# Other PSUM banks for the attention behind the decode's small products, and later squares of the first half's attention result

## The chip, the core and the metric

The kernel runs on one core of one Trainium2 chip. Five engines work side by side, each through its own instructions in order: TensorE (PE, with its weight loads shown apart as PEld), VectorE (DVE), ScalarE (ACT), GpSimd (POOL) and SyncE (SP), which here only issues transfers. Matrix products are written to PSUM, eight banks of 128 x 512 words of 32 bits; the other engines read them from there. The metric is the device time of one execution in microseconds. The program has been measured in several runs, and one more execution was recorded by the profiler.

## The reference

One layer of a decoder that mixes two kinds of heads. It serves a prompt of 1024 tokens and, with the same weights, 8 samples of one token each, whose past of 8192 tokens lies in paged caches. All is in 32-bit floats, D is 1024, there are 8 attention heads of 64.

```python
def fox_attend(q, k, v, cq, ck, qpos, kpos):
    s = jnp.einsum('bqhd,bkhd->bhqk', q, k).astype(jnp.float32) * (ATT_HEAD_DIM ** -0.5)
    s = s + (cq.astype(jnp.float32).transpose(0, 2, 1)[:, :, :, None]
             - ck.astype(jnp.float32).transpose(0, 2, 1)[:, :, None, :])
    s = jnp.where(kpos[None, :] <= qpos[:, None], s, -jnp.inf)
    p = jax.nn.softmax(s, axis=-1).astype(v.dtype)
    return jnp.einsum('bhqk,bkhd->bqhd', p, v)
...
def merge_heads(att, sgu, g_att_out, g_sgu_out, w_o):
    return jnp.concatenate([rmsnorm(att, g_att_out), rmsnorm(sgu, g_sgu_out)], axis=-1) @ w_o
```

Ahead of this stand the projections to q, k, v, a forget logit (its running sum is cq and ck) and the gating heads; behind it stand the cross-attention to 256 memory tokens and a gated MLP with a short convolution. The samples do the same with `fox_attend` over their cached keys and values. The change touches the attention of the prompt, the first norm in `merge_heads`, and the places in PSUM of three small products of the samples' attention.

## The kernel before

**Two streams.** The prompt's work is written as generators that yield a cost; after each yield the main loop deals out pieces of the samples' work (`decode`, then `sample_rest`) at a pace set for each phase. So the samples' instructions lie between the prompt's. A scheduler of the language then places the instructions on the engines; `tc.issue_after(x)` and the helper `behind(engine)` say behind which instruction something has to stand. `lastexp[0]` is the newest exponential of the attention.

**Phases.** First the projections (to about 260 us); then the attention of the first 512 rows (`att0`, to about 372 us), dealt together with the memory's keys and values and the gating of the first half; then the attention of the second 512 rows (`att1`, to about 505 us); then, for each half, the output projection, the cross-attention and the MLP, with the rest of the decode beside them; at the end the rest of the samples' layer.

**One attention.** `attention(hf)` runs over four pairs of heads, two blocks of 256 rows each. `setup` brings q and k of a pair into the form that the products need: it loads qn (L733), k and v (L739, L740) and, in the second half, the keys of the first half from `ks_d` (L769, L770); transposes (L750, L779), copies on ScalarE (L757, L784) and differences on VectorE (L774, L788) follow. `setup` of a pair runs during the pair before; the first pair of the second half is set up within the first attention. `scores` makes the score rows of 128 queries (L807, L809, L811) in a ba bank, their maximum on VectorE (L816; L813 in the first half) and the exponential on ScalarE (L817; L814). `turn` transposes the probabilities (L836) and copies them back (L843, or L841 on VectorE). `values` multiplies by v (L852) and copies the result (L861); `back` transposes that (L872), and VectorE divides it by the sum of the exponentials (L863, L874) into the tile `att`.

**PSUM.** Of the eight banks four are `ba` (in the second attention two tiles of two banks), two `bb`, one `ms` and one `dv`. A tile of a tag waits until the last reader of the tile that had its bank is done. `B3` gives the tiles of `turn`, `values` and `back`: each third goes to `ms`, the others to `bb`. The matrix products of the memory use `ba` and, for each third tile, `bb`. The decode's small products all go to `ms`: the gates' cumulative sum (`gates`, L1409, read by VectorE in L1411), the transpose of the maxima (`soft_all`, L1459, read in L1462) and the spread of the maximum (`soft_exp`, L1472, read in L1474 before the exponential L1475).

**The end of an attention.** `close` is a generator in three steps: the squares of the four 128 x 512 tiles of `att`, summed by ScalarE (`ssq_into`, L230); the reciprocal root (`rstd_of`, VectorE L222, GpSimd L223); and the multiplication of the four tiles by it (VectorE, L958) with two stores to `an_d` on SP's queue (L960). `beside` runs a generator and takes one step of another behind its yields of given numbers. The first half's `close` is begun directly behind the first attention, and its two other steps stand behind the yields 0 and 2 of the second attention. The output projection of the first half reads `an_d` (`merge_in`), which the second attention calls at its fourth pair of heads.

Of the kernel before, what the change touches and what calls it, by code (L numbers as in the profile page):

```python
# [63 lines left out]
M3 = 3  # L64
# [14 lines left out]
def build(nc, tc, ctx, a, phases=None):  # L79
# [27 lines left out]
    def nm(s):  # L107
        cnt[0] += 1
        return f"{s}_{cnt[0]}"
# [16 lines left out]
    def sm(shape, tag, bufs=2, dt=F32):  # L126
        return small.tile(shape, dt, tag=tag, bufs=bufs, name=nm(tag))
# [13 lines left out]
    def BB():  # L141
        return psum.tile([P, 512], F32, tag="bb", bufs=2 + MB, name=nm("bb"))
# [8 lines left out]

    def MS():
        return BB() if MB else psum.tile([P, 512], F32, tag="ms", bufs=1, name=nm("ms"))

    def DV():
        return psum.tile([P, 512], F32, tag="dv", bufs=1, name=nm("dv"))
# [69 lines left out]
    def ssq_into(dst, src):  # L226
        n = src.shape[-1]

        j = src if n > 512 else tpool.tile([P, 512], BF16, tag="junk", bufs=1, name=nm("junk"))[: src.shape[0], :n]
        nc.scalar.activation(j, src, AF.Square, accum_out=dst)  # L230
# [495 lines left out]
    def attention(hf, late=None, at=3):  # L726
        nk = 4 * (hf + 1)
        att = []
# [94 lines left out]
        turns = [0.0, 0]  # L823

        def B3():
            turns[1] += 1
            return MS() if turns[1] % M3 == M3 - 1 else BB()

        def turn(p_, pts, n, ii):

# [116 lines left out]
    def close(hf, att):  # L947

        ssa = sm([P, 4], "ssa", 1)
        for i in range(4):  # L950
            ssq_into(ssa[:, i : i + 1], att[i // 2][:, i % 2, :])
        yield
        r = rstd_of(ssa, AW, 4, "ra")
        yield
        for b2 in range(2):
            for i in range(2):
                t = att[b2][:, i, :]
                nc.vector.tensor_scalar(t, t, r[:, b2 * 2 + i : b2 * 2 + i + 1], None, op0=ALU.mult)  # L958
            t0 = hf * 4 + b2 * 2
            nc.sync.dma_start(an_d[t0 * P : (t0 + 2) * P, :].rearrange("(c p) d -> p c d", p=P), att[b2])  # L960
        yield

    def beside(main, steps, at):

        n = 0
        while True:
            try:
                t = next(main)
            except StopIteration as e:
                return e.value  # L970
            yield t
            if n in at:
                next(steps)
            n += 1
# [381 lines left out]
    lastexp = []  # L1356
# [3 lines left out]
    def behind(e):  # L1360

        return tc.issue_after(last[e]) if e in last else nullcontext()


    def decode():
# [36 lines left out]
        def gates(b, A):  # L1402
            tot = sm([P, 8], "tot", 2)
            nc.vector.tensor_tensor(
                tot, A.rearrange("p (h k) -> p h k", k=64)[:, :, 63], lfz[:, b * 8 : b * 8 + 8], op=ALU.add
            )
            ps = MS()
            with behind(ENG.PE):
                mmul(ps[:, :8], suf, tot, start=True, stop=True)  # L1409
            dt_ = dec("dec").rearrange("p (k h) -> p k h", h=8)  # L1410
            nc.vector.tensor_tensor(  # L1411
                dt_, ps[:, :8].unsqueeze(1).broadcast_to((P, 64, 8)), A.rearrange("p (h k) -> p k h", k=64), op=ALU.subtract
            )
            return dt_
# [39 lines left out]
            return pm  # L1454

        def soft_all(b, pm):
            ps = MS()
            with behind(ENG.PE):
                nc.tensor.transpose(ps[:8, :P], pm, ident)  # L1459
            with tc.high_priority():  # L1460
                m1 = sm([8, 1], "m1", 2)
                nc.vector.tensor_reduce(m1, ps[:8, :P], axis=AX.X, op=ALU.max)  # L1462
                nc.vector.tensor_tensor(mT[:, b : b + 1], m1, snT[:, b : b + 1], op=ALU.max)
                dg = dgs[b % 2]
                nc.vector.tensor_scalar(dg[:8, :], ident[:8, :8], mT[:, b : b + 1], None, op0=ALU.mult)
            return dg

        def soft_exp(b, st, dg):
            s = st[1]
            ps = MS()  # L1470
            with behind(ENG.PE):
                mmul(ps[:, :8], ones, dg, start=True, stop=True)  # L1472
            with tc.high_priority():
                nc.vector.tensor_tensor(s, s, ps[:, :8].unsqueeze(1).broadcast_to((P, 64, 8)), op=ALU.subtract)  # L1474
                nc.scalar.activation(s, s, AF.Exp)  # L1475
                nc.vector.tensor_reduce(lps[:, b, :], s.rearrange("p k h -> p h k"), axis=AX.X, op=ALU.add)
# [366 lines left out]
    def prompt():  # L1843
        def fill():
            yield from pmem()
            if not G0R:
                yield from gating(0)

        got, ahead = [], []
        att1 = attention(1, lambda: got.append(merge_in(0)))  # L1850
        att0, fill0 = attention(0, (lambda: next(att1)) if LT < 4 else None, LT), fill()

        def early():
            next(att0)
            next(fill0)

        yield from p1(early)
        phase[0] = "att0"
        att = yield from mix(att0, fill0, MIXR)
        def load_x(hf):  # L1860
            xt = []
            for i in range(4):
                t = U([P, D])
                nc.sync.dma_start(t, a["x"][(hf * 4 + i) * P : (hf * 4 + i + 1) * P, :])
                xt.append(t)
            return xt

        if LT > 3:
            yield next(att1)
        ending = close(0, att)  # L1870
        next(ending)
        phase[0] = "att1"
        ba_pool(True)
        if G0R:
            att = yield from mix(gating(0), att1, 1 / G0R)
        else:
            att = yield from beside(att1, ending, (0, 2))
        ba_pool(False)
        ending = close(1, att)
        next(ending)  # L1880
        ends = []
        for hf in range(2):
            if not got and hf == 0:
                got.append(merge_in(hf))
            xt = []
            phase[0] = f"mid{hf}"
            if hf == 0:
                mh, ml = yield from beside(merge(*got.pop()), ending, (3, 7))
            else:
                mh, ml = yield from ahead[0]  # L1890
            if ends:
                yield from ends.pop()
            sq = yield from out_proj(a["w_o"], mh, ml, xt, partial(load_x, hf))
            if hf == 0:
                ys = yield from mix(cross(xt, sq), gating(1), 0.05)
            else:
                ys = yield from cross(xt, sq)
            phase[0] = f"ffn{hf}"
            sq = yield from ffn(hf, xt, ys, (lambda: ahead.append(merge(*merge_in(1))) or ahead[0]) if hf == 0 else None)
            held[0] = False  # L1900
            ends.append(final(hf, xt, sq))
        yield from ends.pop()
# [121 lines left out]
```

## Time and profile before

| | |
|---|---|
| Runs, device time | 1807.55, 1807.73, 1808.47 us; median 1807.73 us |
| The profiled execution | 1812.65 us, of which its span is 1810.9 us |
| Granted clock of TensorE, mean of the span | 0.987 |
| Moved | 521.06 MB, mean 288 GB/s |

The profile is of one execution, whose time stands beside its span above: what lies around the span is 1.75 us. The median of the runs is 4.92 us below that execution's time. All times of instructions below are microseconds from the start of the span. In the rows of a timeline the columns are the start, the duration, the engine, the line, the operation and its tiles (result <- operands, buffer numbers left out); a bracket gives how long the engine was idle before and what released it. Rows with x2 or more are neighbouring instructions taken together.

### The profile page before, as it was taken

Reading aid. Unit: us, or ns where it says so; the run is one execution under the profiler, and the core shown is the slowest. Engines: PE = TensorE matmul, PEld = TensorE weight load, DVE = VectorE, ACT = ScalarE, POOL = GpSimd, SP = SyncE. Lnnn points to the kernel's source line nnn. Section 1 sums busy time; section 2 is a strip of 40 time slices with the busy share of each in tenths; the row PEclk is TensorE's granted clock in tenths of the full one; section 3 lists DMA queues with packets and bytes.
Section 4 is the critical chain, followed back from the end, with each engine's and each line's share of the span. In section 5 each row is a group of like instructions: output and inputs, shape, how many; then the busy total and the mean of one; then the engine's idle time right before and its main releaser. Section 6 shows DMA issues by size and latency. Waiting matters only on the chain.

```text
span 1810.9 us, 25097 instructions
## 1 busy us (share of the span) xinstructions
PE 1741.1 (96%) x9637; PEld 1295.4 (72%) x9637; DVE 1398.3 (77%) x1729; ACT 735.3 (41%) x1378; POOL 503.7 (28%) x461
## 2 busy tenths in 40 slices
PE   8999999878999899999999999999989999999997
PEld 5887776656677667777777777766676678767775
DVE  4689668987788887999999899888875549855344
ACT  6332265465633544433323244235353323232332
POOL 1252333522133323233232132433322111001110
PEclk9999999988999999999999999999999999999999
DMA  8886889786596876689788788979878677568982
GB/s 300 305 296 228 303 303 341 251 276 195 214 403 259 344 306 269 261 285 342 298 293 320 291 310 309 382 286 361 315 273 318 241 278 263 182 262 292 360 313 82
DMA packets 157074, 521.06 MB, mean 288 GB/s; under 512 B 20874, under 2 KB 40842, under 8 KB 124186
## 3 DMA queue, kind: packets, MB, share of 16 engines
q0 software_dynamic: 57168, 341.14, 49.7%
q1 hardware_dynamic: 92874, 165.73, 26.5%
q10 hardware_dynamic: 6912, 12.59, 1.8%
q8 instruction: 76, 1.25, 0.3%
q14 instruction: 44, 0.36, 0.1%
HBM read 495.47 MB, written 23.93 MB: 287 GB/s over the span
## 4 chain that ended last, share of the span: by engine, by line
PE 50%; issue 8%; DMA 8%; DVE 7%; POOL 2%; ACT 1%; POOLq 0%; DVEq 0%; ACTq 0%
PE ba L272 6%; PE ba L274 6%; PE ba L273 6%; DMA kv<-cache_v,io 6%; PE dv L1487 3%; PE bb L272 3%; PE bb L273 3%; PE bb L274 3%; DVE s L1439 1%; DVE kv L1435 1%; DVE wl L236 1%; PE dv L331 1%; DMA kv<-cache_k,io 1%; PE dv L1763 1%; POOL kv L1419 1%
## 5 line engine op out<-in xcount | busy, mean ns | idle before, releaser
L235 ACT ACTIVATE wh<-wr 128x1024 fp32r<-128x1024 f32 (+2 forms) x220 | 228.2, 1043 | 451.2 <-PE ba L273 143.2
L236 DVE TENSOR_TENSOR wl<-wr,wh 128x1024 fp32r<-128x1024 f32 (+2 forms) x220 | 263.1, 1202 | 173.8 <-PE ba L274 57.1
L1419 POOL DMA_INDIRECT kv<-cache_k,io x128 | 196.7, 1537 | 578.5 <-DVE s L1439 323.1
L1435 DVE TENSOR_TENSOR kv<-kv,d 128x1024 f32<-128x1024 f32 (+1 forms) x156 | 258.1, 1682 | 32.6 <-DMA kv<-cache_k,io 27.3
L1439 DVE TENSOR_REDUCE s<-kv 128x16 f32<-128x1024 f32 (+1 forms) x156 | 258.6, 1676 | 0.0
L1481 POOL DMA_INDIRECT kv<-cache_v,io x128 | 167.6, 1310 | 258.7 <-PE dv L1487 179.9
L273 PE MATMUL ba<-u,wh 128*128 128x512 f32 x528 | 208.5, 395 | 2.4 <-DVE u L239 2.4
L272 PE MATMUL ba<-u,wh 128*128 128x512 f32 x528 | 209.5, 397 | 0.0
L274 PE MATMUL ba<-u,wl 128*128 128x512 f32 x528 | 209.1, 396 | 0.0
L272 PE MATMUL ba<-wh,u 128*128 128x512 f32 (+1 forms) x495 | 186.1, 379 | 0.9 <-ACT u L235 0.9
L273 PE MATMUL ba<-wl,u 128*128 128x512 f32 (+1 forms) x495 | 185.2, 375 | 1.3 <-DVE wl L236 1.3
L274 PE MATMUL ba<-wh,u 128*128 128x512 f32 (+1 forms) x495 | 183.4, 375 | 0.0
L1487 PE MATMUL dv<-kv,s 128*32 128x512 f32 x1024 | 123.9, 598 | 4.8 <-DMA kv<-cache_v,io 4.8
L274 PEld LDWEIGHTS ba<-u,wl 128*128 128x128 f32 x528 | 99.2, 188 | 29.1 <-issue 5.7
L273 PEld LDWEIGHTS ba<-u,wh 128*128 128x128 f32 x528 | 99.3, 188 | 27.0 <-DVE u L239 2.6
L272 PEld LDWEIGHTS ba<-u,wh 128*128 128x128 f32 x528 | 99.5, 189 | 25.7 <-issue 4.0
L272 PEld LDWEIGHTS ba<-wh,u 128*128 128x128 f32 x495 | 93.0, 188 | 25.0 <-issue 6.5
L272 PE MATMUL bb<-u,wh 128*128 128x512 f32 x272 | 108.5, 399 | 0.0
L273 PE MATMUL bb<-u,wh 128*128 128x512 f32 x272 | 108.0, 397 | 0.0
L274 PE MATMUL bb<-u,wl 128*128 128x512 f32 x272 | 107.9, 397 | 0.0
L273 PEld LDWEIGHTS ba<-wl,u 128*128 128x128 f32 x495 | 93.0, 188 | 20.3 <-DVE wl L236 2.1
L274 PEld LDWEIGHTS ba<-wh,u 128*128 128x128 f32 x495 | 92.9, 188 | 19.4 <-issue 1.6
(444 smaller groups left out, 3330.5 us busy)
## 6 DMA issues: line engine op xcount, KB each, us to landing
wr<-w_up SPq DMA_DIRECT2D x88, 512.0 KB
kv<-w_up POOLq DMA_DIRECT2D x22, 1024.0 KB
wr<-w_down SPq DMA_DIRECT2D x40, 512.0 KB
kv<-w_down POOLq DMA_DIRECT2D x11, 1024.0 KB
wr<-w_in SPq DMA_DIRECT2D x16, 512.0 KB
wr<-w_o SPq DMA_DIRECT2D x16, 512.0 KB
wr<-w_cq SPq DMA_DIRECT2D x16, 512.0 KB
wr<-w_co SPq DMA_DIRECT2D x16, 512.0 KB
```

Source lines behind the costliest of these rows:

```text
L235: nc.scalar.activation(h, src, AF.Copy)
L236: nc.vector.tensor_tensor(l, src, h.bitcast(F32), op=ALU.subtract)
L272: mmul(out, sh, mh, start=(i == 0), stop=False)
L273: mmul(out, sh, ml, start=False, stop=False)
L274: mmul(out, sl, mh, start=False, stop=(i == n - 1))
L331: mmul(ps[32 * j : 32 * j + 32, :w], xT[:, k, :] if nk == 8 else xT[:, k * 8 : k * 8 + 32], raw[:, q, j * w : (j + 1) * w], start=(k == 0) ...
L1419: nc.gpsimd.indirect_dma_start(kv, None, a["cache_k"], off(kidx[:, b, ch : ch + 1]))
L1435: nc.vector.tensor_tensor(kvv[:, i : i + m, :], kvv[:, i : i + m, :], qb.unsqueeze(1).broadcast_to((P, m, 512)), op=ALU.mult)
L1439: nc.vector.tensor_reduce(s[:, ch * 4 + i : ch * 4 + i + m, :].rearrange("p k h -> p (k h)"), kvv[:, i : i + m, :].rearrange("p k (h d) -> ...
L1481: nc.gpsimd.indirect_dma_start(kv, None, a["cache_v"], off(kidx[:, b, ch : ch + 1]))
L1487: mmul(dv[32 * j : 32 * j + 32, :], s[:, ch * 4 : ch * 4 + 4, :].rearrange("p k h -> p (k h)"), kvv[:, j, :], start=(ch == 1), stop=(ch == ...
L1763: mmul(ps[32 * j : 32 * j + 32, :P], xsT[:, k, :], rvs[j // 2][:, k, j % 2, :], start=(k == 0), stop=(k == 7), tile_position=(0, 32 * j),)
```

## The change

There are two edits. The first sets a counter: each of the three small products of the decode takes its bank through `MSD`, which sets `small_[0]` to 2, and `B3`, when the turn of `ms` comes, gives a `bb` tile instead and lowers the counter as long as it isn't zero. The counter works at the time the program is written, not on the chip, and it is not reset between phases. The second moves the squares of the first half: they are written behind the second attention's first yields instead of ahead of it, and each has to stand behind the exponential that is the newest at that point; the two other steps of `close` move from the yields 0 and 2 to 2 and 4. `close` is the same function for the second half, where the squares still are begun directly behind the attention and get the same order behind its last exponential.

```diff
+    small_ = [0]
+
+    def MSD():
+        small_[0] = 2
+        return MS()
...
         def B3():
             turns[1] += 1
-            return MS() if turns[1] % M3 == M3 - 1 else BB()
+            if turns[1] % M3 == M3 - 1:
+                if not small_[0]:
+                    return MS()
+                small_[0] -= 1
+            return BB()
...
     def close(hf, att):
 
         ssa = sm([P, 4], "ssa", 1)
-        for i in range(4):
-            ssq_into(ssa[:, i : i + 1], att[i // 2][:, i % 2, :])
+        with tc.issue_after(lastexp[0]):
+            for i in range(4):
+                ssq_into(ssa[:, i : i + 1], att[i // 2][:, i % 2, :])
         yield
...
         def gates(b, A):
...
-            ps = MS()
+            ps = MSD()
...
         def soft_all(b, pm):
-            ps = MS()
+            ps = MSD()
...
         def soft_exp(b, st, dg):
             s = st[1]
-            ps = MS()
+            ps = MSD()
...
         ending = close(0, att)
-        next(ending)
         phase[0] = "att1"
         ba_pool(True)
...
-            att = yield from beside(att1, ending, (0, 2))
+            att = yield from beside(att1, ending, (0, 2, 4))
```

## The prediction

> **What bounds the kernel now.** I read the page's totals first, then the table of windows by stage, then the waits of TensorE in the two attentions, and last the timeline around each edit.
>
> ```profile
> span 1810.9 us, 25097 instructions
> PE 1741.1 (96%) x9637; PEld 1295.4 (72%) x9637; DVE 1398.3 (77%) x1729; ACT 735.3 (41%) x1378; POOL 503.7 (28%) x461
> PE 50%; issue 8%; DMA 8%; DVE 7%; POOL 2%; ACT 1%; POOLq 0%; DVEq 0%; ACTq 0%
> ```
>
> TensorE is busy 96% of the span and holds half of the chain that ended last, so a microsecond taken from TensorE's idle time should come off the end. The windows say where idle time is (columns: window, its us, busy us and count of PE, PEld, DVE, ACT, POOL, granted clock, DMA share, GB/s).
>
> ```profile
> 260.00:372.00 112.00, 101.79 (x601) 75.25 (x600) 94.89 (x177) 66.08 (x160) 44.87 (x60) 0.97 0.83 290
> 372.00:505.00 133.00, 118.37 (x787) 82.36 (x787) 103.88 (x171) 79.24 (x160) 33.27 (x44) 0.93 0.69 227
> 505.00:1448.00 943.00, 916.80 (x4495) 673.97 (x4494) 806.43 (x888) 373.30 (x698) 291.74 (x213) 0.99 0.82 308
> ```
>
> The first attention (260 to 372 us) leaves TensorE idle for 112 − 101.8 = 10.2 us, the second (372 to 505) for 133 − 118.4 = 14.6 us and at a clock of 0.93. Afterwards TensorE is busy 97% (916.8 of 943): nothing there can absorb a gain or a loss, and the instruction order after 505 us is nearly that of before, so I carry every saving or loss of the attentions to the end one to one. The waits of TensorE from 255 to 505 us (wait: us in total, times, longest):
>
> ```profile
> PE ba L807 <- ACT wr L817: 5.8, 5, 1.9
> PE ms L852 <- DVE dec L1411: 2.7, 1, 2.7
> PE ms L852 <- DVE s L1474: 1.2, 1, 1.2
> ```
>
> The largest is not the change's: scores wait for a buffer that an exponential frees. The turn to other banks can reach only waits of the ms bank, of which the two largest are 2.7 and 1.2 us.
>
> **The change part by part.** It adds and removes no instruction: the counts on every engine are those of before, so all of its price is waits and order. By the order of the changed kernel, eight tiles go from ms to bb, all in the first attention: a pair behind the product left over from the projections (274 us), and pairs behind gates (313), soft_all (338) and soft_exp (366). In the second attention the same tiles keep ms.
>
> *Gates.* The values product wants ms while VectorE still has to read it:
>
> ```profile
> 314.08 0.38 ACT L843 ACTIVATE t<-bb 128x256 f32<-128x256 f32 x1
> 315.13 1.02 DVE L1411 TENSOR_TENSOR dec<-ms,d 128x512 f32<-128x512 f32 x1
> 316.18 1.41 DVE L774 TENSOR_TENSOR u<-ba,u 64x512 fp32r<-64x512 f32 x2
> 316.21 0.87 PE L852 MATMUL ms<-t,u 128*64 128x256 f32 x8 [2.72 <-DVE dec L1411]
> 318.34 0.48 PE L272 MATMUL ba<-wh,u 128*128 128x512 f32 x1
> ```
>
> On bb the product may start when the copy of its operand ends, 314.08 + 0.38 = 314.46, so 1.75 us earlier. But VectorE works without a gap through L1411 into L774, which no bank turn moves, and the gemm L272 needs the ba bank that L774 frees at 316.18 + 1.41 = 317.59. The idle time moves there: what is left is 318.34 − 317.59 = **0.75 us saved** (ends: 0, and the whole 2.72).
>
> *soft_exp.* Its read L1474 is the next:
>
> ```profile
> 361.11 2.36 DVE L678 TENSOR_SCALAR wr<-wr,r4r 128x512 f32<-128x512 f32 x4
> 366.75 0.50 ACT L843 ACTIVATE u<-bb 128x384 f32<-128x384 f32 x1
> 368.28 0.87 PE L852 MATMUL ms<-t,u 128*64 128x256 f32 x8 [1.21 <-DVE s L1474]
> 369.72 0.69 PE L872 MATMUL bb<-cp,t 128*128 128x128 f32 x2 [0.57 <-ACT t L861]
> ```
>
> TensorE is free at 368.28 − 1.21 = 367.07, the operand at 366.75 + 0.50 = 367.25: **1.0 us saved**. At best the 0.57 in front of the back product goes too (1.8); at worst the four L678, which the new order puts in front of maxima, cost about 1 us of their 2.36.
>
> *soft_all.* Here the other operand is as late as the bank:
>
> ```profile
> 337.51 0.60 ACT L843 ACTIVATE u<-bb 128x512 f32<-128x512 f32 x1
> 337.79 0.28 DVE L1462 TENSOR_REDUCE m<-ms 8x1 f32<-8x128 f32 x1 [0.17 <-PE ms L1459]
> 338.12 1.76 PE L852 MATMUL ms<-u,u 128*64 128x256 f32 x16 [0.37 <-DVE m L1462]
> 340.84 0.49 DVE L874 TENSOR_TENSOR u<-bb,rl 128x128 f32<-128x128 f32 x2 [1.21 <-PE bb L872]
> 340.88 0.33 PE L836 MATMUL bb<-cp,t 128*128 128x128 f32 x1
> ```
>
> The copy ends at 338.11, L1462 at 338.07, so the 0.37 stays, hidden by nothing. The bb banks are now asked for once more: the transposes behind the back product must wait for L874, 340.84 + 0.49 = 341.33, and began at 340.88: **0.45 us lost** (ends: 0 and 0.5).
>
> *The left-over pair.* It meets a memory gemm's result in bb:
>
> ```profile
> 273.98 0.69 ACT L720 ACTIVATE t<-bb,rm 128x512 f32<-128x512 f32 x1 [0.33 <-PE bb L274]
> 274.31 0.27 PE L836 MATMUL bb<-cp,t 128*128 128x128 f32 x1
> ```
>
> That bank is free at 273.98 + 0.69 = 274.67 instead of being used at 274.31: **0.36 us lost** (ends 0 and 0.4).
>
> *The squares.* Before, two of four run in ScalarE's gaps at the end of the first attention and one stands directly ahead of the first exponential:
>
> ```profile
> 377.37 0.82 DVE L816 TENSOR_REDUCE mx<-ba 128x1 f32<-128x640 f32 x1
> 378.11 0.63 ACT L230 ACTIVATE junk<-u 128x512 bf16<-128x512 f32 x1
> 378.65 0.18 ACT L230 ACTIVATION_READ_ACCUMULATOR junk<-u 128x1 f32 x1
> 378.74 0.78 ACT L817 ACTIVATE wr<-ba,mx 128x640 f32<-128x640 f32 x1
> 382.75 1.67 DVE L958 TENSOR_SCALAR u<-u,rar 128x512 f32<-128x512 f32 x4
> 387.79 1.08 DVE L816 TENSOR_REDUCE mx<-ba 128x1 f32<-128x896 f32 x1
> ```
>
> The first maximum (L816) is ready at 377.37 + 0.82 = 378.19, so the first exponential gains 378.74 − 378.19 = 0.55. In return the squares stand among the first exponentials, where ScalarE is what scores wait for, and the four L958 go from before the fourth maximum to directly before the fifth (the 128x896 above). I trace the fifth maximum some 1.0 us later (1.67 less the gap that they leave earlier). **Net 0.45 us lost**; ends: 0.55 gained, or four squares at 0.63 + 0.18 in full, 3.2 lost. The rstd on GpSimd (L223) is moved past a gather; nothing waits for it but L958.
>
> *The clock.* Idle TensorE is also slow TensorE here:
>
> ```profile
> 360.00:372.00 12.00, 9.55 (x65) 7.18 (x65) 10.84 (x23) 7.83 (x24) 4.29 (x6) 0.90 0.98 343
> 372.00:385.00 13.00, 10.49 (x61) 7.96 (x61) 8.03 (x16) 8.31 (x21) 2.17 (x3) 0.83 0.35 115
> ```
>
> The 12 us to 372 lose (1 − 0.90) × 12 = 1.2 us to the clock, with 12 − 9.55 = 2.45 us idle; soft_exp's wait is half of that idle time, so I take half: **0.6 us saved** (ends 0 and 1.2). The next 13 us lose (1 − 0.83) × 13 = 2.2 us, which I leave, as the waits for exponentials in it stay.
>
> *Sum:* −0.75 − 1.0 + 0.45 + 0.36 + 0.45 − 0.6 = −1.1 us. The profiled execution lasts 1812.65 us, 1.75 more than its span; −1.1 makes it 1811.55. The median of the runs is 4.92 lower, and there it is 1807.73 − 1.1 = **1806.6 us**. The lower ends add up to −2.72 − 1.8 − 0.55 − 1.2 = −6.3 (1801.5), the upper ones to 1.0 + 0.5 + 0.4 + 3.2 = +5.1 (1812.8). A measurement tells about 0.2% (3.6 us) from no change, so faster means under 1804.1 and slower over 1811.3.
>
> **The rivals.**
>
> *The clock comes back (faster).* If the shorter stalls at 366 to 372 and the earlier first exponential let the clock stay up, the rest of the 1.2 + 2.2 us returns, 3.4 − 0.6 = 2.8 us: 1806.6 − 2.8 = **1803.8 us**. For it: both windows with a low clock are those with the edits. Against it: in the second, the wait on exponentials is untouched.
>
> The Trainium skill ("TensorE: Matmul & The Clock Gate", "Part 1: The HAM clock gate") says that activity releases the throttle; the clock of 0.83 in the window with 2.5 us idle agrees. The same page ("A second HAM failure mode: psum-queue depth-cycling") says that cycling through PSUM banks makes micro-idles that throttle it again; by that the clock would give nothing, 1807.2 instead of 1806.6. No run here shows it for bb yet.
>
> *The stores land late (slower).*
>
> ```profile
> 383.67 1.16 SPq L960 DMA_DIRECT2D an_d<-u  x2
> 385.00:400.00 15.00, 13.20 (x91) 8.03 (x89) 14.66 (x25) 8.41 (x17) 8.31 (x11) 1.00 1.07 295
> 390.46 0.54 SPq L770 DMA_DIRECT2D u<-ks_d  x1
> 397.54 0.48 DVE L874 TENSOR_TENSOR u<-bb,rl 128x128 f32<-128x128 f32 x2
> 907.92 11.30 DMA kv<-cache_v,io
> 1335.27 3.50 DMA wr<-w_up
> ```
>
> In SP's queue the two stores of L960 now stand behind the next head pair's qn load and six ks_d loads, so they leave not at 383.67 but after the last L770, at 391.0. The first L874 of the second attention writes into the place that the first store reads. The trace has no such store on the path: the nearest transfers take 3.5 us (a 512 KB load, as large as a store) to 11.3 us (a gather in full queues), which lands it at 394.5 to 402.3. From 6.5 us on (397.54) it decides: VectorE is in order, and behind L874 stand the decode's products, the next maxima, and so exponentials and scores. At 402.3 this costs 4.8 us, and a stall like that of 372 to 385 another 2.2 of clock: 1806.6 + 7.0 = **1813.6 us**. For it: the DMA engines are full there (share 1.07). Against it: the row of equal size is far below 6.5.
>
> *ScalarE and VectorE pay the squares in full.* 3.2 instead of 0.45: **1809.3 us**. For it: scores' largest wait is for exponentials; against it: ScalarE is busy 79 of 133 us there.
>
> *It does not do what it says.* Only four pairs turn, and if each wait reappears at the next operand and the squares are neutral: **1807.7 us**.
>
> **How the numbers follow.** Forecast 0.30, clock 0.30, stores 0.15, squares 0.13, nothing 0.12. The forecast's own range is 1804.2 to 1810.0. Faster takes 0.28 of the clock, 0.03 of the forecast and 0.03 of the rest, 0.34; slower takes 0.13 of the stores, 0.06 of the squares and 0.05 of the others, 0.24; the same is 0.42. The range for 8 in 10 goes from the sum of the lower ends, 1801.5, to that of the upper ones, 1812.8, and leaves out some 0.08 below and 0.10 above.
>
> **What would show it.** Right: the 2.7 and 1.2 us waits of L852 on L1411 and L1474 are gone, L272 behind the gates starts at L774's end, the clock of 360 to 372 rises to about 0.95, and the fifth maximum of the second attention is about a microsecond later. The stores' rival shows as a wait of the first L874 on a DMA of an_d; the squares' rival as waits of L807 on L817 of well over 5.8 us in all; the clock's as 372 to 385 over 0.95. I am wrong if the time after 505 us changes by more than 1 us, or if the waits behind gates and soft_exp stay.

## The result and the profile after

The changed kernel takes 1820.84 us (median of 8 runs, 1811.97 to 1825.52), the kernel before beside it 1807.87 (8 runs, 1805.09 to 1809.99): a ratio of 1.0071, with a 95% interval of [1.0056, 1.0086], some 13 us slower. The prediction was 1806.6 us with a range up to 1812.8, and no measurable change as the likeliest.

The profiled execution of the change lasts 1824.86 us, 1.86 more than its span. From its page, the span, the busy times and the chain that ended last:

```profile
span 1823.0 us, 25091 instructions
PE 1748.8 (96%) x9637; PEld 1298.0 (71%) x9637; DVE 1399.7 (77%) x1729; ACT 734.1 (40%) x1378; POOL 500.7 (27%) x461
PE 47%; DMA 9%; DVE 8%; issue 7%; ACT 2%; POOL 2%; POOLq 0%; DVEq 0%; SPq 0%; ACTq 0%
```

The busy instructions of every engine are as many as before; 12.1 us of span have come without work. The windows of the changed kernel, with the columns of before. The last two are the stretches in which the work stands that before does at 360 to 372 and 372 to 385 us, as it comes some 8 us later here:

```profile
260.00:372.00 112.00, 97.08 (x559) 69.60 (x558) 85.62 (x159) 59.39 (x142) 41.87 (x57) 0.95 0.76 259
372.00:505.00 133.00, 117.40 (x781) 81.67 (x780) 109.17 (x183) 80.56 (x172) 35.26 (x46) 0.92 0.69 229
505.00:1448.00 943.00, 917.87 (x4487) 672.04 (x4486) 804.99 (x885) 373.41 (x697) 290.66 (x214) 0.98 0.82 310
368.00:380.00 12.00, 10.62 (x73) 6.36 (x66) 10.09 (x20) 7.42 (x23) 6.30 (x9) 1.00 0.75 247
380.00:393.00 13.00, 10.10 (x59) 7.84 (x59) 10.05 (x20) 8.89 (x23) 1.50 (x2) 0.82 0.47 164
```

The first attention does 42 fewer matmuls in its 112 us (x559, before x601), with 4.7 us less of TensorE's busy time. The waits of TensorE from 255 to 505 us say where:

```profile
PE ba L813 <- ACT wr L823: 8.9, 6, 3.9
PE ms L862 <- ACT u L853: 6.4, 3, 5.2
PE bb L846 <- ACT t L820: 4.1, 2, 3.2
```

The two waits of the values product on VectorE (2.7 and 1.2 us before) are gone. New are one of 5.2 us of a values product for a copy on ScalarE and one of 3.2 us of a transpose for an exponential, and the scores' wait for exponentials has grown from 5.8 to 8.9 us.

To see where time goes I matched TensorE's instructions (the n-th of a line in one profile with the n-th of the same line in the profile of before) and took the median difference of their starts in stretches of before's time. I call it the lag, in us:

```
stretch of before      280   305   345   377   415   520  1207  1277  1400
the change            -0.6   5.7   9.7   7.7   8.4   8.4   8.5  16.2  12.3
```

Three losses: 6.3 us at 295, 4.0 at 330, 7.7 at 1260. Between 345 and 377 the lag falls by 2.0, and between 1277 and 1400, most of it near 1350, by 3.9. That last fall is no merit of the change: all twelve experiments, whatever they change, show one of 2.7 to 6.8 there. It lies in before's own profiled execution, which was 4.8 us above the median of its runs: from 1300 to 1360 us its clock is 0.94 (0.97 to 1.00 in the others) and TensorE is idle for 4.6 us (0.6 to 2.4 in the others). From its windows:

```profile
1300.00:1360.00 60.00, 55.37 (x289) 42.58 (x289) 43.98 (x58) 26.15 (x55) 17.83 (x15) 0.94 0.74 281
```

**The loss at 295 us.** On the timeline of ScalarE in the changed kernel:

```profile
291.74 0.69 ACT L726 ACTIVATE t<-ba,rm 128x512 f32<-128x512 f32 x1 [0.34 <-PE ba L280]
297.78 1.06 ACT L241 ACTIVATE wh<-wr 128x1024 fp32r<-128x1024 f32 x1 [5.35 <-DMA wr<-w_cv]
298.74 0.58 ACT L853 ACTIVATE u<-ms 128x512 f32<-128x512 f32 x1
```

ScalarE waits 5.35 us for a weight tile (w_cv) that it has to split, and in its order the copy L853 of the probabilities stands behind that split; TensorE's values product waits for the copy. Before, the same split ran without a wait:

```profile
293.06 1.06 ACT L235 ACTIVATE wh<-wr 128x1024 fp32r<-128x1024 f32 x1
```

Why the weight is late is on GpSimd's and SP's timelines. Before:

```profile
277.71 0.96 POOL L1481 DMA_INDIRECT kv<-cache_v,io  x1 [0.30 <-issue]
278.66 0.58 POOL L771 DMA_DIRECT2D u<-ck_d  x1
...
288.82 1.47 POOL L1419 DMA_INDIRECT kv<-cache_k,io  x1 [2.70 <-DVE mx L813]
290.60 0.97 POOL L1419 DMA_INDIRECT kv<-cache_k,io  x1 [0.30 <-DVE wl L236]
...
289.45 5.61 SPq L249 DMA_DIRECT2D wr<-w_cv  x4
```

And after:

```profile
277.69 0.55 POOL L777 DMA_DIRECT2D u<-ck_d  x1
...
279.57 1.02 POOL L1492 DMA_INDIRECT kv<-cache_v,io  x1 [0.30 <-issue]
...
287.38 1.01 POOL L1430 DMA_INDIRECT kv<-cache_k,io  x1 [0.30 <-issue]
288.70 0.97 POOL L1430 DMA_INDIRECT kv<-cache_k,io  x1 [0.30 <-DVE wl L242]
...
288.70 4.48 SPq L255 DMA_DIRECT2D wr<-w_cv  x4
```

A gather of `cache_v` has moved behind three small loads. The two gathers of `cache_k` then start 1.4 and 1.9 us earlier, both no later than the first load of w_cv, where before one started 0.63 us ahead of it and one 1.15 us behind it. With both gathers ahead of it the load takes 297.78 − 288.70 = 9.1 us; before it was there at 293.06 at the latest, 3.6 us after its issue. The gathers start earlier, as I read the semaphores of these transfers, because a gather has to wait until the transfer that used its semaphore before has landed: in the changed order that is a small load (the semaphore of the first gather is complete at 286.2) and no longer the gather of `cache_v` (288.0). This reading was not varied by itself.

**The loss at 1260 us** starts on VectorE. Before, the lines that matter (VectorE, then GpSimd):

```profile
1217.41 1.22 DVE L236 TENSOR_TENSOR wl<-wr,wh 128x1024 fp32r<-128x1024 f32 x1
1218.54 0.27 DVE L1462 TENSOR_REDUCE m<-ms 8x1 f32<-8x128 f32 x1
1218.74 2.34 DVE L1435 TENSOR_TENSOR kv<-kv,d 128x1024 f32<-128x1024 f32 x2
...
1227.60 2.36 DVE L1435 TENSOR_TENSOR kv<-kv,d 128x1024 f32<-128x1024 f32 x2 [1.79 <-DMA kv<-cache_k,io]
...
1217.76 1.68 POOL L1419 DMA_INDIRECT kv<-cache_k,io  x1 [0.46 <-DVE s L1439]
```

After:

```profile
1226.17 0.27 DVE L1473 TENSOR_REDUCE m<-ms 8x1 f32<-8x128 f32 x1
1226.37 2.34 DVE L1446 TENSOR_TENSOR kv<-kv,d 128x1024 f32<-128x1024 f32 x2
1228.64 1.21 DVE L242 TENSOR_TENSOR wl<-wr,wh 128x1024 fp32r<-128x1024 f32 x1
...
1230.98 1.20 DVE L1450 TENSOR_REDUCE s<-kv 128x16 f32<-128x1024 f32 x1
...
1239.46 2.36 DVE L1446 TENSOR_TENSOR kv<-kv,d 128x1024 f32<-128x1024 f32 x2 [4.88 <-DMA kv<-cache_k,io]
...
1226.53 5.35 POOL L1430 DMA_INDIRECT kv<-cache_k,io  x1 [1.59 <-DVE m L1473]
```

The split of a weight (L236, now L242) has moved behind two products. Before, a short reduction (L1462) followed it while GpSimd was issuing the gather of the next keys. Now that reduction (L1473) is begun 0.36 us before the gather, and VectorE runs two products, two splits and one tiny instruction, all with two operands, back to back until the next reduction at 1230.98. The gather takes 5.35 us instead of 1.68, and in both cases it ends 0.90 us after the start of the first reduction that begins behind its own start. VectorE then waits 4.88 us for the keys instead of 1.79, and TensorE some 26 us later, at 1265.63, 2.64 us for `cache_v` (L1498). The Trainium skill ("GPSIMD Engine Reference", "1. Specifications") says that GpSimd shares its SBUF interfaces with VectorE, with contention where VectorE's instruction has two SBUF inputs; these rows agree with it, and the page gives no price.

### The profile page after: what moved, and what is told of

Its sections match the earlier page's. It is cut to its first block, busy times and chain, and to the rows that moved or that the text cites. A ratio compares the mean times of both kernels' runs of the same rounds, so it can differ in the third digit from the quotient of the medians.

```text
span 1823.0 us, 25091 instructions
## 1 busy us (share of the span) xinstructions
PE 1748.8 (96%) x9637; PEld 1298.0 (71%) x9637; DVE 1399.7 (77%) x1729; ACT 734.1 (40%) x1378; POOL 500.7 (27%) x461
## 4 chain that ended last, share of the span: by engine, by line
PE 47%; DMA 9%; DVE 8%; issue 7%; ACT 2%; POOL 2%; POOLq 0%; DVEq 0%; SPq 0%; ACTq 0%
PE ba L278 6%; PE ba L280 6%; DMA kv<-cache_v,io 6%; PE ba L279 6%; PE dv L1498 3%; PE bb L278 3%; PE bb L279 3%; PE bb L280 3%; DVE kv L1446 2%; DVE s L1450 2%; DMA kv<-cache_k,io 2%; PE dv L337 1%; PE ba L1075 1%; PE ba L1077 1%; PE ba L1076 1%
## 5 line engine op out<-in xcount | busy, mean ns | idle before, releaser
L242 DVE TENSOR_TENSOR wl<-wr,wh 128x1024 fp32r<-128x1024 f32 (+2 forms) x220 | 263.2, 1202 | 165.7 <-PE ba L280 57.8
L1498 PE MATMUL dv<-kv,s 128*32 128x512 f32 x1024 | 127.4, 613 | 6.8 <-DMA kv<-cache_v,io 6.8
```

What stands on the lines that cost most here:

```text
L242: nc.vector.tensor_tensor(l, src, h.bitcast(F32), op=ALU.subtract)
L1498: mmul(dv[32 * j : 32 * j + 32, :], s[:, ch * 4 : ch * 4 + 4, :].rearrange("p k h -> p (k h)"), kvv[:, j, :], start=(ch == 1), stop=(ch == ...
```

## The experiments

All ran in five rounds beside the kernel before on the same chip. The times are medians; the ratios to the kernel before, with a 95% interval, are taken over all runs and can differ a little from the ratio of two medians. For each run the span and the mean granted clock are known, so it can be split by an estimate: span x clock is what would be left at full clock, the rest is lost to the clock. As the clock has three digits and a stretch of waiting can be shorter or longer at another clock, the two parts trade against each other; the sum is safer. "At full clock" and "clock" below are differences of means to the kernel before, in us, with a standard error.

**First: which edit.** The change was taken apart: the bank turns alone, the squares alone, and both without the pair behind the left-over product. The edits are shown against the changed kernel.

*e1, the turns without the second edit:*

```diff
-        with tc.issue_after(lastexp[0]):
-            for i in range(4):
-                ssq_into(ssa[:, i : i + 1], att[i // 2][:, i % 2, :])
+        for i in range(4):
+            ssq_into(ssa[:, i : i + 1], att[i // 2][:, i % 2, :])
...
+        next(ending)
...
-            att = yield from beside(att1, ending, (0, 2, 4))
+            att = yield from beside(att1, ending, (0, 2))
```

> Only the bank turns; the squares as before. Theory A (the pair left over from the projections, turned at 274 us, reorders the schedule behind it, so that two gathers of cache_k leave 0.0 to 1.3 us ahead of the w_cv load and hold it; ScalarE's split of it blocks the copies behind it): the stall near 295 us is there as in the changed kernel (TensorE idle about 5 us before a values product), and the kernel is 6 to 13 us slower than before. Theory B (the squares and the stores cause the loss): no loss, 1805 to 1809 us. Theory C (the second third of the program has runs that differ by chance): 1808 plus or minus 3 us, and the stall at 295 is not always there.

Measured: 1814.48 us, 1.0019 [1.0008, 1.0031]; the lag rises from 0.5 to 8.1 at 295. The stall belongs to the turns. But the kernel is only 3.5 us slower, not the 6 to 13 expected.

*e2, the squares without the turns:* each `MSD()` is `MS()` again.

```diff
-            ps = MSD()
+            ps = MS()
```

> Only the squares and the steps of the close; all banks as before. Theory A: no stall near 295 us, since nothing before 372 us changes much; 1806 to 1811 us. Theory B: slower by 6 to 13 us, with the loss between 372 and 405 us.

Measured: 1809.37 us, 0.9988 [0.9976, 0.9999]; no stall at 295. From 345 to 415 the lag goes from 0.2 to 0.5, over −2.5 at 394 and +3.4 at 398. The squares alone cost nothing: theory B is out.

*e3, the turns without the left-over pair and without the second edit:* the old `close` as in e1, and the counter is put back to zero where the first attention begins.

```diff
+        small_[0] = 0
```

> The bank turns with the counter set to 0 where the first attention begins, so that the pair at 274 us keeps ms; the squares as before. Theory A: the order up to the gates (313 us) is that of before, the stall near 295 us is gone, 1805 to 1810 us. Theory B: like before too. If the bank turns behind gates, soft_all and soft_exp themselves cost the time: slower by 3 us or more, with the loss at 313 to 372 us.

Measured: 1812.52 us, 1.0008 [0.999, 1.0025]; lag 0.2 at 280 and 0.4 at 305, so no stall. It is −3.2 at 415.

*e4, the whole change without the left-over pair:* that line alone, against the changed kernel.

```diff
+        small_[0] = 0
```

> The whole change, with the counter set to 0 where the first attention begins. Theory A: the stall near 295 us is gone, and 6 us or more of the 13 us with it: 1805 to 1812 us. Theory B: as slow as the change, near 1820 us.

Measured: 1810.02 us, 1.0003 [0.9988, 1.0019]; lag −0.4 at 280 and at 305. One line that takes away the first of four pairs, costed at 0.36 us, takes away the whole loss of the change.

**Second: is it the gather?** The theory now was that the left-over pair does harm by the order of GpSimd's queue alone. So the late gather was put into the kernel before, and taken out of the changed one; the change was run again beside them.

*e5, the kernel before with that gather behind the small loads:*

```diff
+                smalls[:] = [newest(ENG.Pool)]
...
+            vcount[0] += 1
+            with tc.issue_after(smalls[0]) if vcount[0] == 10 else nullcontext():
+                nc.gpsimd.indirect_dma_start(kv, None, a["cache_v"], off(kidx[:, b, ch : ch + 1]))
```

> The kernel before, with one instruction moved: the second gather of cache_v near 277 us stands behind the three small loads (ck_d, cq_d, ck_d) on GpSimd's queue instead of ahead of them, as in the changed kernel; no bank and no square moves. Theory A (the gathers of cache_k then leave early, because the DMA semaphores that they reuse are free once the small loads land, and hold the w_cv load that leaves just behind): the two cache_k gathers start near 287.5 and 288.8 us instead of 288.8 and 290.6, the w_cv load lands about 9 us after its issue instead of 3.6, TensorE idles 5 us near 295, and the kernel is 3 to 10 us slower. Rival D (the order of ScalarE's and VectorE's instructions near 290 us makes the stall, the gathers are only carried along): no stall, within 3 us of before.

Measured: 1821.39 us, 1.0053 [1.0032, 1.0074]. No bank is turned here, and the stall is there; on ScalarE's timeline:

```profile
296.82 1.06 ACT L235 ACTIVATE wh<-wr 128x1024 fp32r<-128x1024 f32 x1 [4.43 <-DMA wr<-w_cv]
```

The `cache_k` gathers start at 285.68 and 287.00, w_cv is issued at 288.42, and the lag goes from −0.8 to 5.2. Up to 308 us this gather is the one instruction that has another place on any engine, so its order makes the stall by itself. From there on the order differs at other places too, the split at 1217 us among them, so the whole time is not the gather's alone.

*e6, the changed kernel with a higher priority for that gather:*

```diff
+            with tc.high_priority() if vcount[0] == 10 else nullcontext():
+                nc.gpsimd.indirect_dma_start(kv, None, a["cache_v"], off(kidx[:, b, ch : ch + 1]))
```

> The whole change, with that one gather put back ahead of the small loads by its priority; TensorE, VectorE, ScalarE and SyncE keep the changed kernel's order, on GpSimd a few later transfers move as well. Theory A: the cache_k gathers start near 288.5 and 290, the w_cv load lands within 5 us, the wait of 5.2 us of the values product near 295 is gone; 5 to 10 us faster than the change, so 1810 to 1816 us. Rival D: the wait stays, near 1820 us.

Measured: 1826.51 us, 1.0076 [1.0056, 1.0096]. A miss: the priority moved no instruction, so this is the change once more, and it says nothing on the gather.

*e7, the change again, unedited:*

> The changed kernel once more, for a second profile on the same chip. Theory A: the stall of 5 us near 295 is there again, lag at 505 us of 7 to 10 us against before. Theory C (chance in the later part): the lag after 505 us, which was 12 us at the end of the first profile, differs from that by more than 2 us.

Measured: 1827.1 us, 1.0065 [1.0041, 1.0089]. The stall is there again, but the lag at 520 us is 12.5, over the 7 to 10 expected, and 15.4 at 1400 instead of 12.3: theory C, that the later part differs by over 2 us from one execution to the next, holds beside A. With e6 it makes 12 runs of one order: +9.2 ± 1.4 us at full clock and +4.5 ± 1.7 by the clock.

**Third: the gather put back, and parts.**

*e8, the changed kernel with the three small loads written behind the gather:*

```diff
+    def later(hold, load):
+        if hold:
+            smalls.append(load)
+        else:
+            load()
...
+            vcount[0] += 1
+            if vcount[0] == 10:
+                with tc.issue_after(newest(ENG.Pool)):
+                    while smalls:
+                        smalls.pop(0)()
```

> The whole change, with the second gather of cache_v near 277 us ahead of three of the small loads on GpSimd's queue, as in the kernel before; the order on the four other engines is the changed kernel's, instruction for instruction. Theory A: the two cache_k gathers start near 288.5 and 290 us, the w_cv load that ScalarE's split waits for lands in about 4 us, the wait of about 5 us of the values product near 295 us is gone, and 5 to 7 us of the lag at 505 us go; what is left of the lag is the loss near 330 us (3 us). Time 4 to 9 us below the changed kernel. Rival D: the wait stays, no change against the changed kernel.

Measured: 1819.94 us, 1.0064 [1.0041, 1.0088]. The stall is gone, with the order on the other four engines that of the change:

```profile
292.93 1.06 ACT L242 ACTIVATE wh<-wr 128x1024 fp32r<-128x1024 f32 x1 [0.17 <-DMA wr<-w_cv]
```

The lag is −0.3 at 280 and at 305. But the ratio hardly falls, where 4 to 9 us less were expected: at full clock it is +5.3 ± 0.8 (the change +9.2 ± 1.4), while the clock loses 5.8 ± 2.2. So the gather is not all of it; what e8 still has are the losses at 330 and at 1260.

*e9, only the left-over pair, with the old `close`:* the counter is set in the first phase alone.

```diff
-        small_[0] = 2
+        small_[0] = 2 * (phase[0] == "p1")
```

> Only the pair left over from the projections turns (274 us); no pair behind the products of the first attention, the squares as before. Theory A: this alone moves the gather, so the stall near 295 us and the loss near 330 us are there, lag 6 us at 300 and 8 to 9 at 345 us; slower than before by 0.2 to 0.7%. If the stall needs the other turned pairs: no stall, within 0.1% of before.

Measured: 1815.57 us, 1.0034 [1.0018, 1.005]; the lag goes from 0.0 to 7.2 at 295. Two tiles turned at 274 us are enough for the stall, and for some 6 us of time by the ratio.

*e10, only the soft_exp pair, with the second edit:* `MS()` in the gates and in `soft_all`, and the counter is zero at the start of the first attention.

```diff
-            ps = MSD()
+            ps = MS()
...
+        small_[0] = 0
```

> The squares as in the change; of the bank turns only the pair behind soft_exp (366 us). Theory A: no stall near 295; the saving of about 1 to 2 us at 366 us adds to that of the squares; 0.1 to 0.3% faster than before. Rival: like before within 0.1%, as the later part swallows it.

Measured: 1807.17 us, 0.9999 [0.9987, 1.0011]. No stall, and no gain in time: the rival's figure.

**Fourth: the gather at 1218 us.** By now the profiles showed two kinds. In seven (the change, e3, e5 to e8, and later e11) the `cache_k` gather there takes 5.34 to 5.35 us, in the others 1.68. So the split was moved by itself in the kernel before (e11), and in the changed kernel a reduction was put between the products (e12).

*e11, the kernel before with that one split behind the products:*

```diff
+        wcount[0] += 1
+        with tc.issue_after(marks[0]) if wcount[0] == 142 else nullcontext():
+            split(raw, h, l)
...
+                if (b, ch) == (7, 1):
+                    marks[:] = [newest(ENG.DVE)]
```

> The kernel before, with one instruction of VectorE moved: a weight's split near 1217 us stands behind the products of the next cache_k tile, as the changed kernel has it. Theory E (with the split gone, the gather of cache_k that leaves just then meets four two-operand instructions of VectorE in a row; GpSimd needs 5.3 us for it instead of 1.7, the keys come late, and TensorE loses 4 to 8 us between 1250 and 1275): that gather takes 5.3 us, VectorE waits about 5.5 us for its data instead of 1.8, lag of 5 to 8 us against before at 1270 us and of 3 to 5 at 1360; slower by 0.1 to 0.4%. Rival F (chance of the DMA, not this order): gather at 1.7 us, no lag, within 0.1%.

Measured: 1811.02 us, 1.0017 [1.0006, 1.0029]. From its trace, GpSimd's gather and TensorE's wait:

```profile
1223.89 5.34 POOL L1423 DMA_INDIRECT kv<-cache_k,io  x1 [2.84 <-DVE m L1468]
...
1262.45 1.92 PE L1493 MATMUL dv<-kv,s 128*32 128x512 f32 x16 [3.50 <-DMA kv<-cache_v,io]
```

The moved split alone makes the long gather (beside it, only a few products on TensorE just behind it have another place), and the lag goes from 4.5 (1207) to 9.2 (1277). The runs show 3.1 us of it.

*e12, e8 with, in addition, the products and sums of that tile in turn and two splits behind the first of them:*

```diff
+        wcount[0] += 1
+        with tc.issue_after(marks[0]) if wcount[0] in (142, 143) else nullcontext():
+            split(raw, h, l)
...
+            if (b, ch) == (7, 1):
+                prev = last[ENG.DVE]
+                for i in range(0, 4, m):
+                    with tc.issue_after(prev):
+                        nc.vector.tensor_tensor(
...
+                        nc.vector.tensor_reduce(
...
+                    prev = newest(ENG.DVE)
+                    marks.append(prev)
+                return 1
```

> The whole change with two repairs: the second gather of cache_v near 277 us ahead of the small loads (as in the run with the gather ahead), and near 1218 us a reduction of VectorE, which reads one operand, between the products of the cache_k tile, with two of the splits behind it. Theory A and E: no wait near 295 us, the cache_k gather near 1218 us takes 2 to 3 us instead of 5.3, the loss at 1255 to 1275 us is gone, and what is left is the 3 us near 330 us: within 0.3% of before, 6 us or more below the change. Rival F: the loss at 1255 to 1275 stays at 5 to 8 us, and the time is that of the run with the gather ahead, 0.6% above before.

Measured: 1813.64 us, 1.0023 [1.0009, 1.0037]. On the timelines of VectorE and GpSimd:

```profile
1223.94 1.22 DVE L1464 TENSOR_REDUCE s<-kv 128x16 f32<-128x1024 f32 x1
...
1231.72 2.36 DVE L1475 TENSOR_TENSOR kv<-kv,d 128x1024 f32<-128x1024 f32 x2 [0.18 <-DMA kv<-cache_k,io]
...
1222.86 1.87 POOL L1443 DMA_INDIRECT kv<-cache_k,io  x1 [1.60 <-DVE m L1502]
```

With a sum (one operand) between the products the gather takes 1.87 us, VectorE waits 0.18 us for the keys, and the lag doesn't rise: 4.9 at 1207, 4.6 at 1277. Against e8 the order differs at this place alone (with a few products of TensorE beside it), and the ratio falls from 1.0064 to 1.0023. The clock is higher as well; the first row is of the change, the second of e12:

```profile
1250.00:1300.00 50.00, 43.97 (x189) 26.81 (x188) 41.73 (x49) 33.16 (x87) 16.76 (x12) 0.90 0.78 291
```

```profile
1250.00:1300.00 50.00, 46.96 (x225) 28.52 (x225) 46.47 (x52) 28.59 (x71) 17.70 (x15) 1.00 0.83 307
```

The lower clock is not always there: of the seven with the long gather it is 0.90 to 0.93 in the change, e6 and e8, where the lag rises by 7.7 to 8.4, and 0.97 to 1.00 in e3, e5, e7 and e11, where it rises by 3.6 to 4.7.

**All together.** The rise of the lag at the three places, in us, and which of the two orders each kernel has:

```
                 late v gather   280->305   305->345   long k gather   1207->1277
the change            yes           6.3        4.0          yes            7.7
e6                    yes           6.7        4.0          yes            7.9
e7                    yes           8.1        4.0          yes            3.6
e1                    yes           7.6        4.0          no            -0.7
e9                    yes           7.2        2.0          no            -0.1
e5                    yes           6.0        1.1          yes            4.6
e8                    no            0.0        4.8          yes            8.4
e12                   no            0.3        4.0          no            -0.3
e3                    no            0.2        0.1          yes            3.6
e4                    no            0.0        0.1          no             0.2
e2                    no            0.7       -0.3          no            -0.2
e10                   no            0.3        0.9          no            -1.2
e11                   no            0.1        0.0          yes            4.7
```

The two orders part the thirteen profiles without an exception. Both mended (e12), 1.0071 becomes 1.0023: 0.0048 of 1808 us, some 9 of 13 us, with about 4 us of uncertainty by the two intervals. The rest, some 4 us, is as large as the column in the middle, but no run takes that loss out.

**What stays open.** The 4.0 to 4.8 us at 330 are there in all six kernels that have both the left-over pair and the other turns, 2.0 with the left-over pair alone (e9), and 0.1 without it (e3, e4). The trace of the change shows VectorE's maximum L819 late (the first row), behind sums and products of the other work, and TensorE's wait for the exponential behind it:

```profile
335.80 0.56 DVE L819 TENSOR_REDUCE mx<-ba 128x1 f32<-128x384 f32 x1
...
337.12 0.86 PE L846 MATMUL bb<-cp,t 128*128 128x128 f32 x3 [3.19 <-ACT t L820]
```

Before, that wait is 1.5 us (at 329.98). That another order on VectorE is the cause is argued from these rows; no run moved that maximum alone. Open, too, is why the squares alone measure nothing (0.9988), the turns alone +3.5 us and both together +13: the orders at 1218 differ (e1 has the short gather), which gives a part, and the clock differs (e1 −3.8 ± 1.0, the change +4.5 ± 1.7), whose choice no run explains. The best version, e2, is 0.1% below the kernel before, with an interval that ends at 0.9999, just clear of no change; e10, which has the same squares, is at 0.9999.

## Why the prediction was wrong

**Gates: right in the wait, not in what follows it.** Predicted 0.75 us saved. In e3, without the stall in front, the product is on `bb` and waits for its copy alone:

```profile
313.29 0.34 PE L1419 MATMUL ms<-tot,cp 128*128 128x8 f32 x2
...
314.93 0.87 PE L862 MATMUL bb<-t,u 128*64 128x256 f32 x8 [1.03 <-ACT t L853]
...
316.39 0.55 PE L846 MATMUL bb<-cp,t 128*128 128x128 f32 x3 [0.58 <-ACT t L820]
...
317.71 0.48 PE L278 MATMUL ba<-wh,u 128*128 128x512 f32 x1
```

The small product stood at 312.88 before (0.41 later here) and the gemm at 318.34 (0.63 earlier here): 1.04 us saved. But what limits it is not L774, as the prediction had it: the gemm starts at 317.71, before that line (L780 here) ends at 318.01, and the new wait is for an exponential (0.58). And the saving doesn't last: at 330 TensorE waits 2.6 us for the exponential L820 in e3 and e4, 1.5 before, and the lag of e3 goes from −0.6 back to 0.7.

**soft_exp: right, and rather more than predicted; its clock isn't shown.** Predicted 1.0 us (1.8 at best) and 0.6 of clock. The lag falls near 367 us, by 2.1 in e3 (0.3 to −1.8) and in e4, and by 1.2 to 1.3 in the change and in e10. That is the wait and not the clock, as before's slow stretch only begins at 369.6 (its clock is 1.00 from 360 to there). From 370 to 377 e3 gains nothing more, though its clock stays at 1.00. And e2, which turns no bank, has that clock too:

```profile
360.00:372.00 12.00, 9.53 (x72) 6.75 (x69) 11.06 (x23) 8.04 (x24) 4.51 (x7) 1.00 0.96 333
```

All nine profiles with this pair turned have 1.00 in that stretch of the work; of the five without, e2 and e5 have it as well, and before, e9 and e11 have 0.89 to 0.91. So the turn may raise the clock, but the 0.6 us are in none of these lags.

**soft_all and the direct cost of the left-over pair: not seen.** From 332 to 340 us e3's lag goes from 0.7 to 0.5, where 0.45 were to be lost. At 280 the lag of the kernels with the left-over pair lies between −0.8 and 0.8, so 0.36 can neither be shown nor excluded.

**The squares: right in the sum, in part by luck.** Predicted 0.45 us lost; e2 loses 0.3 from 345 to 415. The two parts are as predicted. The first exponential comes 1.67 us earlier, at 377.07 instead of 378.74; 1.15 of it is the first maximum, which TensorE brings at 376.22 instead of 377.37 in this execution, and 0.52 the squares (predicted 0.55). The fifth maximum starts at 387.76, before at 387.79, so it has lost 1.1 against the first (predicted 1.0). But the lag is −2.5 at 394, and the loss comes behind it, at a place that the prediction doesn't name: the next maximum, of 128x1024, has gone behind five other instructions of VectorE. The first row is of before, the others are of e2:

```profile
395.20 1.22 DVE L816 TENSOR_REDUCE mx<-ba 128x1 f32<-128x1024 f32 x1
...
397.95 1.21 DVE L816 TENSOR_REDUCE mx<-ba 128x1 f32<-128x1024 f32 x1
...
399.20 1.11 ACT L817 ACTIVATE wr<-ba,mx 128x1024 f32<-128x1024 f32 x1 [6.22 <-DVE mx L816]
```

**The rivals.** The stores are late in the queue as their rival said, at 398.74 in the change, but no first L884 waits for them:

```profile
398.74 2.28 SPq L971 DMA_DIRECT2D an_d<-u  x2
```

The squares' rival has its sign, waits of L807 on L817 well over 5.8 us (8.9 in e2 and in the change), but not its price: the longest, 4.6 us in e2, stands behind the late maximum, and e2's 0.9988 [0.9976, 0.9999] excludes 3.2 us more. The clock from 372 to 385 us is 1.00 in the change, which reads like the sign of the clock's rival. But other work stands there: the work that before has at 372 to 385 comes at 380 to 393, at 0.82 as against 0.83. So that clock did not come back.

**The step that failed** is "*The left-over pair.* It meets a memory gemm's result in bb ... **0.36 us lost** (ends 0 and 0.4)". I costed the pair by the wait for its bank alone. What it does is to change the scheduler's order: a gather of `cache_v` goes behind three small loads on GpSimd, and that costs 6 to 8 us at 295 (e5 with it and no turn; e8 without it and with all turns). This pair alone makes the kernel some 6 us slower (e9). Beside that stands the sentence that "the instruction order after 505 us is nearly that of before, so I carry every saving or loss of the attentions to the end one to one". One weight split behind two products at 1218 us was in that "nearly": 4.7 us in e11's trace, up to 8.4 (e8) where the clock falls as well. So the prediction's own sign of being wrong, a change of over 1 us behind 505, is met: 8.4 at 520, 12.3 at 1400. Nor is every loss carried one to one: e1 is 12.1 us behind at 345, 8.7 at 520, and 3.5 slower in its runs. The moved gather and the moved split were both to be seen in the changed kernel's order before it ran. I read the order for the turned tiles and for the squares, and took the other moved instructions for free since their counts were the same. Rivals for "a transfer is issued earlier and starves another" and for "an order far away flips" were missing, so the range had no room for them.

**The clock** was taken as 0.6 us saved; over the whole span of the change's 12 repeated runs it is 4.5 ± 1.7 us lost. The rule of the Trainium skill weighed against it ("TensorE: Matmul & The Clock Gate", "A second HAM failure mode: psum-queue depth-cycling"), that cycling through banks throttles, does not show behind soft_exp: that pair stands near 376 us in the change, and the clock from 368 to 380 us is 1.00.

## What to carry to other kernels

Compare the whole order of the old and the new kernel on every engine and queue, not the edited lines alone, and price each moved transfer and each moved VectorE instruction by what starts beside it; a change that shifts no count can still shift a gather. Ahead of a load that an in-order engine waits for, look which gathers are issued in the microseconds before it. Where GpSimd issues gathers, look whether a reduction stands between VectorE's long instructions with two operands; here it was worth 3.5 us of a gather's issue.

## What the runs showed of the hardware

- The same gather takes 1.68 us on GpSimd where VectorE's two-operand instructions have a short reduction between them, and 5.34 to 5.35 where they run back to back, with so little spread that seven profiles agree to 0.01 us. In all fourteen profiles it ends 0.8 to 0.9 us after the start of the first reduction behind its own start. It is not rare: in the kernel before 8 of 256 gathers of the caches take over 3 us, and the longest, 6.29 us from 110.40, ends 0.9 us after the start of the next reduction, too. Nor is it a law: at 318.58 a gather takes 1.23 us beside three products of 128x512. That the number of operands decides was not varied by itself.
- A 512 KB load issued behind two gathers took 8.4 (e5) to 9.1 us (the change); with one of the gathers behind it, 3.6 (before) and 3.5 (e8).
- The same order can lose different amounts to the clock. Up to 1217 us e11 is the kernel before, instruction by instruction, and yet its execution comes out of the second attention 4.3 us later. The windows, before and then e11:

```profile
420.00:450.00 30.00, 25.11 (x156) 18.58 (x158) 21.33 (x36) 15.58 (x33) 6.81 (x11) 0.83 0.73 217
```

```profile
420.00:450.00 30.00, 25.56 (x132) 18.09 (x131) 20.46 (x31) 14.03 (x27) 8.33 (x13) 0.72 0.65 194
```

One profile against another tells such an amount from no change only where several kernels agree, as in the table above.
